# An RWKV-7 inversion on Trainium2: forward substitution in 8x8 blocks, joined to 16x16 by two products

## The chip, the cores and the metric

The kernel runs on one core of a Trainium2 chip. The metric is device time of one execution in microseconds (us), the median of several runs. The engines are TensorE (PE, its weight loads PEld), VectorE (DVE), ScalarE (ACT), GpSimd (POOL) and SyncE (SP, which issues the DMAs).

## The reference

Two layers of a hybrid decoder over 1024 tokens of width 1024. Each layer projects x, mixes tokens in three groups of heads (stick-breaking attention, latent attention, RWKV-7), projects back, and runs a gated FFN. What the change touches is the RWKV-7 mixer; its recurrence over time is

```python
def rwkv7_mixer(cols, mu, w0, w2, a0, a2, g2, k_k, k_a, r_k, gn_g, gn_b):
...
    def step(state, inp):
        r_t, w_t, k_t, v_t, kk_t, a_t = inp
        sa = jnp.einsum('bhvk,bhk->bhv', state, -kk_t)
        state = (state * w_t[:, :, None, :] + sa[..., None] * (kk_t * a_t)[:, :, None, :]
                 + v_t[..., None] * k_t[:, :, None, :])
        return state, jnp.einsum('bhvk,bhk->bhv', state, r_t)
...
    _, ys = lax.scan(step, init, (tm(rh), tm(wh), tm(kh), tm(vh), tm(kk), tm(ah)))
```

The kernel computes it in chunks of 64 tokens. Inside a chunk the dependence of each `sa` on earlier ones is a 64x64 triangular system, one for each chunk and head. The kernel inverts these unit triangular matrices.

## The kernel before

Matmuls with weights are three products in split precision (`mm3`, L205 to L207): `whi` and `wlo` are the high and low part of a weight tile, made by L200 (ScalarE) and L201 (VectorE).

`phase_a` holds the part around the change. For each of four feature tiles `ft` of 128 features (two heads) it projects k, then r, then v. Such a projection (`proj_rw`) has two halves of 512 tokens; each half is 24 matmuls into a PSUM tile `psmm`, of which there are three buffers, and is evacuated by L306 (ScalarE), then L310 or L308 and L311 (VectorE), which mixes each token with the one before it. L311 is the last large reader of the buffer. `rw_prep` and `rw_stage1` turn k, r, v into the operands of the chunks: L619 scales k, L643 and L644 make the masked operand that L668 transposes, L669 transposes v beside it, L649 and L653 make the operand that L676 transposes, and L689 and L690 mask the products of L684 into `Aa` and `RB`.

After two feature tiles `Aa` holds the A of 64 systems, and `rw_inv` inverts them; there are two such inversions in a layer, four in all. `rw_inv` is a generator. It copies the diagonal 32x32 blocks (L726, two pieces), transposes them so that each partition holds a whole block (L729), and inverts each 32x32 block on VectorE by rows. Before the change, forward substitution runs for t = 1 to 15 on the two 16x16 diagonal blocks at once: `mul` (L731) multiplies row t of A with the rows already known, `red` (L732) sums. Then the 16x16 block below the diagonal is joined by two products in four pieces each (first into `M`, then into `T`). `pd` holds the elementwise products. L752 transposes the result (`T11`), L761 on TensorE starts the join of 32x32 blocks to 64x64, with L780 and L792 after it, and L768 transposes once more.

What sets the order: a scheduler fixes each engine's order from the order of the program's text, with a few shifts of priority per helper. `step(n)` takes n pieces of `rw_inv`, up to its n-th next `yield`, into the text. The first inversion of a layer starts at ft = 2: six pieces after k's projection, six after r's, the rest after v's. The second runs beside `rw_chain(0, ...)`, the recurrence over chunks (L848 to L870), three pieces for each of its steps.

Of the kernel before, what the change touches and what calls it, by code (L numbers as in the profile page):

```python
# [69 lines left out]
class Body:  # L70
# [640 lines left out]
    def rw_inv(self, st, tp, Aa):  # L711
        nc = self.nc
        v32 = lambda t: t.rearrange("p (a b) -> p a b", b=32)
        LA = v32(self.t(tp, [P, S], "LA"))
        T = v32(self.t(tp, [P, S], "T"))
        pd = self.t(tp, [P, S], "pd")
        pd3 = v32(pd)
        M = self.t(tp, [P, 16, 16], "M")
# [11 lines left out]
        blk = lambda ap, off, dims: bass.AP(tensor=ap.tensor, offset=ap.offset + off, ap=[list(ap.ap[0])] + [list(d) for d in dims])  # L730
        mul = lambda o, x, y: nc.vector.tensor_tensor(o, x, y, op=ALU.mult)  # L731
        red = lambda o, x: nc.vector.tensor_reduce(o, x, axis=AX.X, op=ALU.add)  # L732
        for t in range(1, 16):
            pr = pd[:, : 2 * t * t].rearrange("p (b j i) -> p b j i", b=2, j=t)
            mul(pr, blk(LA, t * 32, [[528, 2], [0, t], [1, t]]), blk(T, 0, [[528, 2], [1, t], [32, t]]))
            red(blk(T, t * 32, [[528, 2], [1, t]]), pr)
            if t % 3 == 0:
                yield
        for j0 in range(0, 16, 4):
            ni = 16 - j0  # L740
            pr = pd[:, : 16 * 4 * ni].rearrange("p (t j i) -> p t j i", t=16, j=4)
            mul(pr, blk(LA, 512 + j0, [[32, 16], [0, 4], [1, ni]]), blk(T, j0 * 32 + j0, [[0, 16], [1, 4], [32, ni]]))
            red(M[:, :, j0 : j0 + 4], pr)
            yield
        for t0 in range(0, 16, 4):
            ni = t0 + 4
            pr = pd[:, : 4 * 16 * ni].rearrange("p (t j i) -> p t j i", t=4, j=16)
# [510 lines left out]
```

## Time and profile before

| | |
|---|---|
| median of 3 runs | 3023.79 us (3023.44 to 3026.31) |
| the profiled execution | 3025.69 us, its span 3024.0 us |
| TensorE busy | 2913.1 us (96%) |
| VectorE busy | 1727.8 us (57%) |
| ScalarE busy | 1074.8 us (36%) |
| GpSimd busy | 230.8 us (8%) |

The profile is of one execution. Its page gives busy times, the span in slices and the chain of work that ended last; behind the page stands the trace, in which each instruction has its start, its duration and the idle time before it. The span is 1.69 us shorter than the time of its execution. Busy time is not the time that an engine costs: only where the others wait for it does it lengthen the span. Granted clock is the share of TensorE's full clock.

### The profile page before, as it was taken

How to read it: one execution, taken by the hardware profiler on the slowest of the kernel's cores; microseconds unless marked ns; L12 is line 12 of the kernel's file. 1: busy time of each engine (PE TensorE's matmuls, PEld its weight loads, DVE VectorE, ACT ScalarE, POOL GpSimd, SP SyncE). 2: the span in 40 equal slices, each digit the busy share in tenths (PEclk: the TensorE clock that was granted, in tenths of full speed). 3: DMA queues.
4: the chain of work that ended last, by engine and by line, in shares of the span. 5: the costliest groups of instructions: out<-in, count | busy, mean ns of one | idle time of the engine just before them, and what ended most of it. 6: DMA issues, size and time to landing. Idle time of an engine off the chain costs nothing.

```text
span 3024.0 us, 41845 instructions
## 1 busy us (share of the span) xinstructions
PE 2913.1 (96%) x16572; PEld 2322.0 (77%) x16572; DVE 1727.8 (57%) x2857; ACT 1074.8 (36%) x1833; POOL 230.8 (8%) x308
## 2 busy tenths in 40 slices
PE   8999999889999999999999999999899999999998
PEld 6777777667888888888877777776678888888887
DVE  4568665886544444344645677568965443434437
ACT  5454454762211112121254644457612111212120
POOL 0001122030000000000000011210300000000000
PEclk9999999999999999999999999999999999999999
DMA  4353666324411111111124446562244111111111
GB/s 135 91 157 102 209 193 203 92 82 137 167 56 42 42 43 55 49 56 49 63 77 125 127 133 207 177 213 66 90 145 163 42 42 42 56 49 55 50 49 56
DMA packets 338260, 301.78 MB, mean 100 GB/s; under 512 B 24200, under 2 KB 302992, under 8 KB 338064
## 3 DMA queue, kind: packets, MB, share of 16 engines
q1 hardware_dynamic: 338064, 299.11, 32.6%
q8 instruction: 131, 2.15, 0.3%
q14 instruction: 65, 0.53, 0.1%
HBM read 208.87 MB, written 90.18 MB: 99 GB/s over the span
## 4 chain that ended last, share of the span: by engine, by line
PE 76%; DVE 10%; issue 8%; ACT 3%; DMA 3%; POOL 1%; SPq 0%; POOLq 0%; DVEq 0%; ACTq 0%
PE psmm L207 16%; PE psmm L206 16%; PE psmm L205 16%; PE psps L205 5%; PE psps L206 5%; PE psps L207 5%; PE pspa L848 2%; DVE pd L731 1%; PE pspi L792 1%; PE psmt L216 1%; DMA LA<-xxd 1%; DVE T L732 1%; PE pspa L684 1%; ACT pd L726 0%; DVE mexp L400 0%
## 5 line engine op out<-in xcount | busy, mean ns | idle before, releaser
L207 PE MATMUL psmm<-xTh,wlo 128*128 128x512 f32 x2144 | 849.1, 396 | 0.0
L205 PE MATMUL psmm<-xTh,whi 128*128 128x512 f32 x2144 | 847.0, 395 | 0.0
L206 PE MATMUL psmm<-xTl,whi 128*128 128x512 f32 x2144 | 846.8, 395 | 0.0
L200 ACT CAST whi<-raw 128x1024 fp32r<-128x1024 f32 x152 | 160.0, 1053 | 1062.1 <-PE psmm L206 1048.6
L205 PEld LDWEIGHTS psmm<-xTh,whi 128*128 128x128 f32 x2144 | 404.0, 189 | 88.6 <-issue 6.1
L206 PEld LDWEIGHTS psmm<-xTl,whi 128*128 128x128 f32 x2144 | 404.2, 189 | 87.9 <-issue 4.6
L207 PEld LDWEIGHTS psmm<-xTh,wlo 128*128 128x128 f32 x2144 | 404.2, 189 | 87.6 <-issue 4.2
L201 DVE TENSOR_TENSOR wlo<-raw,whi 128x1024 fp32r<-128x1024 f32 x152 | 185.6, 1221 | 456.7 <-ACT whi L200 440.4
L1060 DVE TENSOR_TENSOR y<-y,psps 128x512 f32<-128x512 f32 x288 | 196.5, 687 | 171.1 <-PE psps L207 171.0
L205 PE MATMUL psps<-wdh,hh 128*128 128x512 f32 x672 | 266.7, 397 | 0.0
L206 PE MATMUL psps<-wdl,hh 128*128 128x512 f32 x672 | 262.9, 391 | 0.0
L207 PE MATMUL psps<-wdh,hl 128*128 128x512 f32 x672 | 259.6, 391 | 0.0
L205 PEld LDWEIGHTS psps<-wdh,hh 128*128 128x128 f32 x672 | 126.1, 188 | 36.8 <-ACT hh L200 5.9
L923 POOL TENSOR_TENSOR lsm<-lsm,small 128x1 f32<-128x1 f32 x32 | 29.3, 915 | 1629.9 <-DVE lsm L922 1629.9
L207 PEld LDWEIGHTS psps<-wdh,hl 128*128 128x128 f32 x672 | 126.2, 188 | 26.9
L206 PEld LDWEIGHTS psps<-wdl,hh 128*128 128x128 f32 x672 | 126.2, 188 | 25.4
L1035 DVE TENSOR_TENSOR cv<-cv,psmm 128x1024 f32<-128x1024 f32 x44 | 53.8, 1222 | 136.6 <-PE psmm L207 131.7
L201 DVE TENSOR_TENSOR wdl<-raw,wdh 128x1024 fp32r<-128x1024 f32 x42 | 51.5, 1226 | 88.2 <-ACT wdh L200 88.2
L1030 ACT ACTIVATE cv<-cv 128x1024 f32<-128x1024 f32 x44 | 46.7, 1061 | 115.8 <-DVE cv L1029 115.8
L848 PE MATMUL pspa<-RBl,PSl 128*128 128x128 f32 x512 | 72.0, 286 | 11.1 <-ACT QC L851 5.3
L848 PEld LDWEIGHTS pspa<-RBl,PSl 128*128 128x128 f32 x512 | 64.6, 195 | 19.3 <-ACT QC L851 8.3
L206 PE MATMUL psmm<-wol,whi 128*128 128x512 f32 x192 | 76.6, 399 | 1.6 <-DVE wol L201 1.6
(444 smaller groups left out, 4504.7 us busy)
## 6 DMA issues: line engine op xcount, KB each, us to landing
raw<-in_ffn_w_up_dram SPq DMA_DIRECT2D x88, 512.0 KB
raw<-in_w_in_dram SPq DMA_DIRECT2D x44, 512.0 KB
raw<-in_ffn_w_down_dram SPq DMA_DIRECT2D x44, 512.0 KB
rbd<-RB SPq DMA_DIRECT2D x64, 256.0 KB
PSl<-psd SPq DMA_DIRECT2D x32, 512.0 KB
RBl<-rbd SPq DMA_DIRECT2D x32, 512.0 KB
psd<-Vz SPq DMA_DIRECT2D x64, 128.0 KB
xxd<-X SPq DMA_DIRECT2D x64, 128.0 KB
```

The lines of the kernel that those rows point to most:

```text
L200: self.nc.scalar.copy(hi, src)
L201: (eng or self.nc.vector).tensor_tensor(lo, src, hi.bitcast(F32), op=ALU.subtract)
L205: mm(out, lh, rh, start=start, stop=False)
L206: mm(out, lh, rl, start=False, stop=False)
L207: mm(out, ll, rh, start=False, stop=stop)
L216: nc.tensor.transpose(pt[:, k * P : k * P + P], xt[:, kk * P : kk * P + P], self.ident)
L684: ms.append(nc.tensor.matmul(pAs[h][:, cc * P : cc * P + P], flat(BK[hr, 2 * g + cc // 2, cc % 2]), AR[hr, :, 2 * g + cc // 2, cc % 2, :], ...
L731: mul = lambda o, x, y: nc.vector.tensor_tensor(o, x, y, op=ALU.mult)
L848: nc.tensor.matmul(pQ[:, f, e, :], PSh[:, f, h, e, :], RBh[:, f, h, e, :], start=True, stop=True)
L1030: nc.scalar.activation(cv, cv, AF.Gelu)
L1035: nc.vector.tensor_tensor(cv, cv, pg, op=ALU.mult)
L1060: nc.vector.tensor_tensor(y[:, i, hs], y[:, i, hs], ps, op=ALU.add)
```

## The change

Substitution runs for t = 1 to 7 on the four 8x8 diagonal blocks at once. Two products then make the 8x8 block below the diagonal in each of the two 16x16 blocks, each product in two halves b (one for each 16x16 block): A's lower left block times the upper inverse into `M`, then the lower inverse times `M` into `T`. The join from 16x16 to 32x32 and all that follows stay. An inversion has 38 instead of 46 multiplies and reductions on VectorE, and 21 instead of 22 pieces: substitution had yields behind t = 3, 6, 9, 12 and 15, and now behind t = 3 and 6 and behind each of the new products. Below the edit lines move down by nine (L752 becomes L761, L761 becomes L770).

```diff
--- before.py
+++ after.py
@@ -730,12 +730,21 @@
         blk = lambda ap, off, dims: bass.AP(tensor=ap.tensor, offset=ap.offset + off, ap=[list(ap.ap[0])] + [list(d) for d in dims])
         mul = lambda o, x, y: nc.vector.tensor_tensor(o, x, y, op=ALU.mult)
         red = lambda o, x: nc.vector.tensor_reduce(o, x, axis=AX.X, op=ALU.add)
-        for t in range(1, 16):
-            pr = pd[:, : 2 * t * t].rearrange("p (b j i) -> p b j i", b=2, j=t)
-            mul(pr, blk(LA, t * 32, [[528, 2], [0, t], [1, t]]), blk(T, 0, [[528, 2], [1, t], [32, t]]))
-            red(blk(T, t * 32, [[528, 2], [1, t]]), pr)
+        for t in range(1, 8):
+            pr = pd[:, : 4 * t * t].rearrange("p (b j i) -> p b j i", b=4, j=t)
+            mul(pr, blk(LA, t * 32, [[264, 4], [0, t], [1, t]]), blk(T, 0, [[264, 4], [1, t], [32, t]]))
+            red(blk(T, t * 32, [[264, 4], [1, t]]), pr)
             if t % 3 == 0:
                 yield
+        prs = [pd[:, 512 * b : 512 * b + 512].rearrange("p (t j i) -> p t j i", t=8, j=8) for b in range(2)]
+        for b in range(2):
+            mul(prs[b], blk(LA, 528 * b + 256, [[32, 8], [0, 8], [1, 8]]), blk(T, 528 * b, [[0, 8], [1, 8], [32, 8]]))
+            red(M[:, 8 * b : 8 * b + 8, 0:8], prs[b])
+        yield
+        for b in range(2):
+            mul(prs[b], blk(T, 528 * b + 264, [[32, 8], [0, 8], [1, 8]]), blk(M, 128 * b, [[0, 8], [1, 8], [16, 8]]))
+            red(blk(T, 528 * b + 256, [[32, 8], [1, 8]]), prs[b])
+        yield
         for j0 in range(0, 16, 4):
             ni = 16 - j0
             pr = pd[:, : 16 * 4 * ni].rearrange("p (t j i) -> p t j i", t=16, j=4)
```

The scheduler's order moves with it. The first place is VectorE in the first inversion of a layer, at ft = 2 of layer 1. `psmm_2031` (`psmm_2029` after) is the second half of r, `psmm_2082` (`psmm_2076`) the first of v, `q_388` the operand of L668, `T_1919`, `M_1921` and `pd_1920` are the inversion's. Before:

```order
L731 TENSOR_TENSOR pd_1920<-LA_1918,T_1919 128x162
L732 TENSOR_REDUCE T_1919<-pd_1920 128x2x9
L731 TENSOR_TENSOR pd_1920<-LA_1918,T_1919 128x200
L732 TENSOR_REDUCE T_1919<-pd_1920 128x2x10
L308 TENSOR_TENSOR pst_2002<-pst_2002,small_15_95 128x1
L311 SCALAR_TENSOR_TENSOR pst_2002<-psmm_2031,pv_67_288,pst_2002 128x511
L731 TENSOR_TENSOR pd_1920<-LA_1918,T_1919 128x242
L619 SCALAR_TENSOR_TENSOR kk_1955<-pst_1861,pv_67_288,kk_1955 128x1024
L732 TENSOR_REDUCE T_1919<-pd_1920 128x2x11
L643 SCALAR_TENSOR_TENSOR q_388_2364<-kk_1955,q_386_2357 128x4x63
L731 TENSOR_TENSOR pd_1920<-LA_1918,T_1919 128x288
L644 TENSOR_SCALAR q_388_2364<-kk_1955 128x4
```

After:

```order
L732 TENSOR_REDUCE T_1919<-pd_1920 128x4x7
L731 TENSOR_TENSOR pd_1920<-LA_1918,T_1919 128x512 x2
L732 TENSOR_REDUCE M_1921<-pd_1920 128x8x8 x2
L731 TENSOR_TENSOR pd_1920<-T_1919,M_1921 128x512 x2
L732 TENSOR_REDUCE T_1919<-pd_1920 128x8x8 x2
L619 SCALAR_TENSOR_TENSOR kk_1953<-pst_1861,pv_67_288,kk_1953 128x1024
L308 TENSOR_TENSOR pst_2000<-pst_2000,small_15_95 128x1
L311 SCALAR_TENSOR_TENSOR pst_2000<-psmm_2029,pv_67_288,pst_2000 128x511
L731 TENSOR_TENSOR pd_1920<-LA_1918,T_1919 128x1024
L310 TENSOR_SCALAR small_15_95<-psmm_2076,pv_67_288 128x1
L732 TENSOR_REDUCE M_1921<-pd_1920 128x16x4
L311 SCALAR_TENSOR_TENSOR pst_2075<-psmm_2076,pv_67_288,pst_2075 128x511
```

Before, t = 11 and later stand behind L311 of r's second half, and v's L311 follows a few rows behind the last one shown. Now both new products and L619 stand ahead of that L311, and a piece of the join to 32x32 stands between it and v's.

The second place is TensorE a little later, at the start of ft = 3. `psmm_2110` (`psmm_2104` after) is the second half of v, `psmm_2620` (`psmm_2612`) the first half of k of the next feature tile, `psmm_2640` the second half of it, `psmm_2718` the first half of r after that. Before:

```order
L207 MATMUL psmm_2110<-xTh_132,wlo_2077 128x512
L668 MATMUL pspa_2393<-ident_65,q_388_2364 128x128
L669 MATMUL pspa_2393<-cent_84,pst_2081 128x128
L668 MATMUL pspa_2393<-ident_65,q_388_2364 128x128
L669 MATMUL pspa_2393<-cent_84,pst_2081 128x128
L205 MATMUL psmm_2620<-xTh_132,whi_2614 128x512
L206 MATMUL psmm_2620<-xTl_133,whi_2614 128x512
L207 MATMUL psmm_2620<-xTh_132,wlo_2615 128x512
```

After:

```order
L207 MATMUL psmm_2104<-xTh_132,wlo_2071 128x512
L205 MATMUL psmm_2612<-xTh_132,whi_2606 128x512
L206 MATMUL psmm_2612<-xTl_133,whi_2606 128x512
L205 MATMUL psmm_2640<-xTh_132,whi_2606 128x512
L206 MATMUL psmm_2640<-xTl_133,whi_2606 128x512
L205 MATMUL psmm_2718<-xTh_132,whi_2712 128x512
L206 MATMUL psmm_2718<-xTl_133,whi_2712 128x512
L668 MATMUL pspa_2385<-ident_65,q_388_2356 128x128
L669 MATMUL pspa_2385<-cent_84,pst_2075 128x128
L668 MATMUL pspa_2385<-ident_65,q_388_2356 128x128
L669 MATMUL pspa_2385<-cent_84,pst_2075 128x128
L207 MATMUL psmm_2612<-xTh_132,wlo_2607 128x512
```

Before, the transposes of L668 and L669 come at once, and then the next k half whole. Now the first two matmuls of three projection halves stand ahead of these transposes, and the products with `wlo` behind them. Layer 2 has the same two pieces of order. Layer 1's attention is also issued in another order than before, layer 2's is not.

## Rows read from the trace of the kernel before

**Rows 1.** Page, chain that ended last: share of the span by engine.
```profile
PE 76%; DVE 10%; issue 8%; ACT 3%; DMA 3%; POOL 1%; SPq 0%; POOLq 0%; DVEq 0%; ACTq 0%
```

**Rows 2.** Windows: length, busy (x) of PE, PEld, DVE, ACT, POOL; PEclk, DMA, GB/s.
```profile
250.00:275.00 25.00, 19.92 (x131) 14.34 (x132) 24.00 (x34) 5.89 (x13) 2.53 (x3) 0.93 0.41 114
...
1750.00:1775.00 25.00, 20.39 (x124) 15.16 (x123) 23.97 (x32) 6.31 (x13) 2.50 (x3) 0.93 0.32 91
```

**Rows 3.** Window of t = 8 to 15, second inversion, tile pd alone.
```profile
359.24:371.10 11.86, 0.00 (x0) 0.00 (x0) 8.77 (x16) 0.00 (x0) 0.00 (x0) 0.99 0.77 269
```

**Rows 4.** VectorE's timeline, second inversion: start, duration, engine, line, operation, out<-in.
```profile
358.60 0.34 DVE L731 TENSOR_TENSOR pd<-LA,T 128x98 f32<-128x98 f32 x1
358.97 0.26 DVE L732 TENSOR_REDUCE T<-pd 128x14 f32<-128x98 f32 x1
...
360.86 0.53 DVE L731 TENSOR_TENSOR pd<-LA,T 128x200 f32<-128x200 f32 x1
361.42 0.36 DVE L732 TENSOR_REDUCE T<-pd 128x20 f32<-128x200 f32 x1
...
379.56 1.08 DVE L731 TENSOR_TENSOR pd<-LA,T 128x512 f32<-128x512 f32 x1
...
383.23 0.68 DVE L732 TENSOR_REDUCE M<-pd 128x64 f32<-128x512 f32 x1
```

**Rows 5.** VectorE's timeline, first inversion of layer 1.
```profile
233.44 0.40 DVE L731 TENSOR_TENSOR pd<-LA,T 128x128 f32<-128x128 f32 x1
...
235.95 0.74 DVE L311 SCALAR_TENSOR_TENSOR pst<-psmm,pv,pst 128x511 f32<-128x511 f32 x1
...
237.13 1.29 DVE L619 SCALAR_TENSOR_TENSOR kk<-pst,pv,kk 128x1024 f32<-128x1024 f32 x1
...
241.17 0.76 DVE L311 SCALAR_TENSOR_TENSOR pst<-psmm,pv,pst 128x511 f32<-128x511 f32 x1
...
242.31 1.23 DVE L201 TENSOR_TENSOR wlo<-raw,whi 128x1024 fp32r<-128x1024 f32 x1
...
247.48 0.75 DVE L311 SCALAR_TENSOR_TENSOR pst<-psmm,pv,pst 128x511 f32<-128x511 f32 x1
248.14 2.08 DVE L731 TENSOR_TENSOR pd<-LA,T 128x1024 f32<-128x1024 f32 x1
...
250.72 1.23 DVE L732 TENSOR_REDUCE M<-pd 128x64 f32<-128x1024 f32 x1
...
272.63 2.12 DVE L752 STREAM_TRANSPOSE LA<-T 128x1024 f32<-128x1024 f32 x1
```

**Rows 6.** TensorE's timeline beside it; brackets: idle time before, releaser.
```profile
243.01 0.40 PE L207 MATMUL psmm<-xTh,wlo 128*128 128x512 f32 x1
...
254.05 0.66 PE L676 MATMUL pspq<-ident,q 128*128 128x128 f32 x4 [3.61 <-DVE q L653]
...
255.75 0.63 PE L207 MATMUL psmm<-xTh,wlo 128*128 128x512 f32 x1
256.17 0.63 PE L205 MATMUL psmm<-xTh,whi 128*128 128x512 f32 x1
...
258.31 0.40 PE L206 MATMUL psmm<-xTl,whi 128*128 128x512 f32 x1
258.54 0.39 PE L207 MATMUL psmm<-xTh,wlo 128*128 128x512 f32 x1
```

**Rows 7.** TensorE's waits, 243 to 288 us: total, times, longest.
```profile
PE pspq L698 <- DVE Aa L689: 0.7, 1, 0.7
PE pspi L761 <- DVE LA L752: 0.5, 1, 0.5
```

**Rows 8.** TensorE's waits, 284 to 352 us.
```profile
PE pspi L792 <- DMA LA<-xxd: 0.9, 1, 0.9
PE pspi L792 <- ACT T L793: 0.7, 1, 0.7
```

**Rows 9.** TensorE's waits, 352 to 440 us (chain 0, second inversion).
```profile
PE pspa L848 <- ACT QC L851: 2.2, 1, 2.2
```

## The prediction

> **What bounds the kernel now.** I read the chain of waits first: TensorE holds 76% of it, VectorE 10% [rows 1]. So the time is TensorE's work plus the places where it stands still, and an edit on VectorE counts only where TensorE waits for VectorE. The table of 25 us windows finds such a place: between 250 and 275 us VectorE is busy for 24.00 of 25 us, TensorE for 19.92 at a granted clock of 0.93, and in layer 2 the same picture stands at 1750 to 1775 [rows 2]. This is where the first inversion of a layer runs beside the projections of feature tile 2 (below: ft 2). TensorE's timeline shows the size: before L676 at 254.05 it idles 3.61 us for VectorE's q (L653), and then its matmuls start 0.42 apart (255.75, 256.17); from 258.31 they start 0.23 apart again (258.31, 258.54) [rows 6]. Of the two clock levels, 1.2 and 2.4 GHz, the first pace is that of the lower one. So some 4.2 us, 254.05 to 258.31, run at about half pace: 2.1 us are lost. Smaller waits follow: 0.7 for Aa (L689), 0.5 for the transposed T11 (L752) [rows 7], 0.9 and 0.7 at L792 [rows 8]. A layer's first inversion thus costs TensorE 3.6 + 2.1 + 0.5 + 0.7 + 1.6 = **8.5 us** now. There are four inversions: two such (one a layer), and two beside the recurrence of chain 0, where the longest wait, 2.2, is for ScalarE's QC [rows 9].
>
> **VectorE's work.** Removed are steps t = 8 to 15: eight multiplies and eight reductions, together 8.77 us [rows 3]. Steps 1 to 7 stay, each over twice the elements. The seventh goes from 98 to 196 elements; at 98 the pair costs 0.34 + 0.26, at 200 it costs 0.53 + 0.36 [rows 4], so this step grows by 0.29. The smaller ones grow by their elements at the same rate (98 elements more for 0.29; the other six add 182 between them, at 0.003 each): 0.55. Growth 0.85, between 0.3 (the last step alone) and 2.0 (seven times the last). Added are four multiplies of 512 elements and four reductions of 512 to 64: 4 x (1.08 + 0.68) = 7.04 [rows 4]. Net per inversion: -8.77 + 0.85 + 7.04 = -0.9, with the gaps of eight instructions fewer about -1.2. Four inversions take about 4.4 us off VectorE, 0.15% of the span. That alone is below 6 us (0.2%), about what a measurement of this kernel can tell from no change.
>
> **What the order moves.** The larger effect is where the new products stand. The first six pieces of the inversion run in step(6), ahead of the evacuations of r and v. Before, they end with t = 12, and the scheduler mixes t = 11 to 15 with the evacuations. Now they are the loading of A, t = 1 to 7 and both new products, and VectorE's order has all 7.04 us ahead of L311 of r's second half, and L619 too. Behind the waiting L311 stand two more evacuations, v's halves, each now behind a large product of the next join (1024 and 768 elements). TensorE needs all three: its new order puts two matmuls of each of the next three projection halves ahead of L668, and each half needs a PSUM buffer that one of the three L311 sets free (there are three). I walk VectorE through this, since it does not pause there. Neighbours overlap by 0.09 (L311 at 247.48 lasts 0.75, its successor starts at 248.14 [rows 5]); small steps between (L310, L643, L644), 0.1 to 0.5 a group, are estimates.
> - r, second half: t = 8 started at 233.44 [rows 5]. From there 0.85 + 7.04 + L619's 1.29 less nine overlaps: L311 at 241.8 instead of 235.95, its end 242.5.
> - v, first half: behind 2.08 + 1.23 (the 1024 pair): L311 at 245.6 instead of 241.17, end 246.4.
> - v, second half: behind the 768 pair, 2.5 by interpolation between the pairs of 512 and 1024, and a small step: 248.9 instead of 247.48, end 249.6.
> - q for L668: behind a 512 pair and three small steps: 251.7; it was ready ahead of wlo's start at 242.31. wlo takes 1.23 and ends at 252.9 instead of 243.5.
>
> TensorE comes free of v's last half at 243.24 (the matmul at 243.01 plus a step). Two matmuls to 243.7, then it waits for 246.4: 2.7. Two to 246.85, waits for 249.6: 2.75. Two to 250.05, waits for 251.7: 1.65. L668 and L669 to 252.15, waits for wlo at 252.9: 0.7. Sum 7.8, in place of 3.6. L653, second half, for which TensorE waited until 254.05, moves to about 259, but now TensorE has 25 matmuls (5.7 us, more at the low clock) ahead of L676, so that wait goes to nothing. What is late next is T11: its transpose ended at 274.75 [rows 5] and will end about 5 us earlier (in the new order the evacuations, the Aa masks of L689 and L690 and one wlo stand behind it), but TensorE's order now has L761 earlier too; I put the wait at 1.1 (as before, 0.5, up to 2), the wait for Aa behind the second transpose at 0.9 (0 to 1.5), those at L792 at 0.8 (0 to 1.6). The low clock I take once, 2.1, since the last idle time is followed by a long row of matmuls as at 254.05. After: 7.8 + 2.1 + 1.1 + 0.9 + 0.8 = 12.7. Less 8.5 gives **+4.2 a layer**, with ends at 2.6 (the later waits gone) and 5.6 (their upper ends, or half of the low clock again).
>
> **The second inversion of a layer** has no projections beside it. Its pieces come three at a time between chunks of chain 0, one piece fewer in all. VectorE's chain is 1.2 shorter; of that TensorE gets what is not covered by the 2.2 for QC, which no edit touches. I take -0.7, between -1.2 (all of it) and +1 (a chunk's evacuation behind a large product, half of a wait like that in rows 9).
>
> Layer 1's attention is also issued in another order by the scheduler; its work is the same. No row prices it: 0, with ends -2 and +2, about the longest single wait seen [rows 9].
>
> **Sum.** 2 x (4.2 - 0.7) = +7.0 us. The profiled execution took 3025.69 (span 3024.0 and 1.69 around it), 1.9 above the median of the runs, so it would become 3032.7, and the median 3023.79 becomes 3030.8. Range of this case: 2 x (2.6 - 1.2) - 2 = +0.8 to 2 x 5.6 + 2 = +13, 3024.6 to 3037.
>
> **Clock.** In the rows one idle time of 3.61 is followed by about 4.2 us at the lower level, and the granted clock of the whole window is 0.93 [rows 2, 6]; no row shows several short idle times in a row. The Trainium skill, page "TensorE: Matmul & The Clock Gate", section "A second HAM failure mode: psum-queue depth-cycling", tells of a kernel that paused briefly each time it cycled through PSUM buffers, so that the clock went up and down and throughput was lost in between. By that section the new waits for three buffers would be paid again in pace, and the sum would be that of rival B; by the row it is the 2.1 that I took.
>
> **Rivals.**
> - **B, the clock stays low.** If TensorE runs from 252.9 to L761 at the lower level, the some 44 large matmuls there lose 0.2 each [rows 6], 8.8 instead of 2.1, while the waits for T11 and Aa (2.0) are covered: +4.7 a layer more, 3030.8 + 9.4 = 3040. For it: three idle times within 10 us. Against: after 3.61 us of idling the pace came back within 4.2.
> - **C, the order moves nothing that counts (faster).** If VectorE gets the evacuations done in time, as it would if the new products overlapped other work, the change does only what its words say: VectorE reaches L653 1.2 earlier, the wait of 3.6 becomes 2.4, T11's 0.5 goes, and about 1 of the 2.1 at the low clock; with the second inversion's 0.7: 2 x 3.4 = 6.8 less, 3017. It decides if L311 of v's first half ends before TensorE needs it, 243.7. Against: VectorE is busy for 24 of 25 us there, and the order is fixed.
> - **D, given back.** The inversion ends about 5 us earlier. If this clears all later waits (T11, Aa, L792), the sum after is 9.9, +1.4 a layer, and the second inversion at its better end gives -1.2: 3024, no change.
>
> **Chances.** Forecast case 0.66 (0.38 of it above 6 us, 0.28 within), B 0.10, C 0.13, D 0.11. Slower by over 0.2%: 0.38 + 0.10 = 0.48; within: 0.28 + 0.11 = 0.39; faster: 0.13. The range 3021 to 3037 leaves out B and most of C, about 2 in 10; the forecast case's own range is 3024.6 to 3037.
>
> **What would show it.** In the profile after: VectorE's busy time some 4 us less; L311 of r's second half near 242 and three waits of TensorE for L311, L311 and L644 of about 2.7, 2.7 and 1.6 between 243 and 252, none for L653; the lower clock only once, around 253 to 257; T11's transpose ending near 270. Wrong would be: waits for L311 under 1 us (then C), matmuls at the 0.42 pace beyond 260 (then B), no waits at L761 and L792 (then D), or a difference that lies in attention, where I put nothing.

## The result and the profile after

The changed kernel takes 3047.01 us in the median (3039.79 to 3050.09), the kernel before 3024.61 beside it (3023.44 to 3026.31). The ratio is 1.0070, interval 1.0051 to 1.0090: slower, and by about three times what was forecast (3030.8, range 3021 to 3037). The profiled execution took 3045.18, its span 3043.4; before it was 3025.69 and 3024.0, so the two traces differ by 19.4 us. The page after, its span, its busy times and its chain of waits by engine:

```profile
span 3043.4 us, 41847 instructions
...
PE 2926.6 (96%) x16572; PEld 2330.4 (77%) x16572; DVE 1723.8 (57%) x2825; ACT 1074.6 (35%) x1833; POOL 233.1 (8%) x308
...
PE 75%; DVE 9%; issue 8%; DMA 3%; ACT 3%; POOL 1%; SPq 0%; POOLq 0%; DVEq 0%; ACTq 0%
```

VectorE is busy 4.0 us less than before (1727.8), as the change meant. TensorE is busy 13.5 us *more* (2913.1 before), with the same 16572 matmuls. That is the line to start from: two thirds of the loss are not waiting but work that takes longer. In the chain, the shares hardly differ from [rows 1].

Was the first inversion as forecast? VectorE's timeline after, the three L311 of [rows 5] (r's second half, v's two halves), q's last piece L644 and the transpose of T11:

```profile
239.65 0.80 DVE L311 SCALAR_TENSOR_TENSOR pst<-psmm,pv,pst 128x511 f32<-128x511 f32 x1
...
243.56 0.74 DVE L311 SCALAR_TENSOR_TENSOR pst<-psmm,pv,pst 128x511 f32<-128x511 f32 x1
...
246.90 0.75 DVE L311 SCALAR_TENSOR_TENSOR pst<-psmm,pv,pst 128x511 f32<-128x511 f32 x1
...
249.52 0.17 DVE L644 TENSOR_SCALAR q<-kk 128x4 f32<-128x4 f32 x1
...
264.77 2.16 DVE L761 STREAM_TRANSPOSE LA<-T 128x1024 f32<-128x1024 f32 x1
```

TensorE's timeline beside it, for comparison with [rows 6]:

```profile
244.45 0.47 PE L205 MATMUL psmm<-xTh,whi 128*128 128x512 f32 x1 [2.81 <-DVE pst L311]
...
247.79 0.77 PE L205 MATMUL psmm<-xTh,whi 128*128 128x512 f32 x1 [2.63 <-DVE pst L311]
...
249.74 0.47 PE L668 MATMUL pspa<-ident,q 128*128 128x128 f32 x1 [0.75 <-DVE q L644]
...
251.50 0.63 PE L205 MATMUL psmm<-xTh,whi 128*128 128x512 f32 x1
251.93 0.63 PE L206 MATMUL psmm<-xTl,whi 128*128 128x512 f32 x1
...
253.05 0.40 PE L206 MATMUL psmm<-xTl,whi 128*128 128x512 f32 x1
253.28 0.40 PE L207 MATMUL psmm<-xTh,wlo 128*128 128x512 f32 x1
...
257.17 0.60 PE L676 MATMUL pspq<-ident,q 128*128 128x128 f32 x4
...
266.99 1.20 PE L770 MATMUL pspi<-LA,Aa 32*32 32x32 f32 x64 [1.12 <-DVE LA L761]
```

The end of v's projection stands 2.2 us earlier here than before (0.3 earlier in `after_again`, a second run of the same program), so 2.2 is to be added: L311 at 241.8, 245.7 and 249.1, L644's last at 251.7. TensorE waits 2.81 and 2.63 for L311 and 0.75 for L644; none is left for L653 (L676 at 257.17 has no bracket). Matmuls start 0.43 apart at 251.50 and 0.23 apart from 253.05: the low clock once. The granted clock is at its lower level from 246.0 to 252.9, and TensorE works for 4.3 us of that (before: from 254.9 to 258.3, 3.4 us, all of it work). T11 makes TensorE wait 1.12.

Then where do 19 us come from? To see it I count the matmuls of projections (psmm from x) in TensorE's timelines, since both kernels have the same ones, and compare the times at which the same number is done. 624 stands at the end of v of ft 2, 850 just ahead of chain 0, 1104 at the last projection matmul of chain 1, 1120 at the start of the FFN, behind attention and the output projection. Differences of after and before over each stretch, in us:

| stretch (projection matmuls) | layer 1 | layer 2 |
|---|---|---|
| 624 to 850, first inversion | +1.2 | +0.4 |
| 850 to 1104, both chains and the second inversion | +10.1 | +7.7 |
| 1104 to 1120, rest of chain 1, attention, output projection | +1.8 | +0.2 |

The rest is the start of layer 1 (2.2 earlier) and of layer 2 (0.2 later). So the loss lies in the second stretch, where I had put -0.7; before, it is 144.4 and 144.5 us long. In layer 2 the work of TensorE in it is the same, in layer 1 it holds 16 more Y products (some 0.9). Of +10.1 in layer 1, waits are 3.0; S and Y products (L867, L875) cost 4.8 more, those 16 among them, projection matmuls 2.4 more, T11 products 0.6 more.

Layer 2 is another mixture. Its stretch, length, busy (x) of PE, PEclk, DMA, GB/s, before and after, and a piece of it after:

```profile
1857.71:2002.17 144.46, 139.21 (x1284) 0.99 0.66 208
```

```profile
1869.25:2021.45 152.20, 144.56 (x1284) 0.97 0.61 192
...
1928.77:1932.18 3.41, 3.41 (x26) 0.50 0.15 55
```

The granted clock is at its lower level for 10.2 us here, in three pieces like the last one, against 3.4 before; at half pace that is 3.4 of the +7.7. Waits are 2.4, and some 2 are left for slower work at the full clock. In layer 1 the clock goes the other way: none at the lower level after, 3.4 us before. Over the whole span the clock is no rival: it is 0.989 in the mean before and 0.986 after, but 0.985 in `x_first` below, which takes no longer than the kernel before.

Back in layer 1, this is TensorE at the same place towards the end of chain 1 in both kernels, after first:

```profile
496.30 0.33 PE L876 MATMUL pspq<-S,QC 128*64 128x64 f32 x2
496.56 0.50 PE L207 MATMUL psmm<-xTh,wlo 128*128 128x512 f32 x1
496.99 0.33 PE L876 MATMUL pspq<-S,QC 128*64 128x64 f32 x2
497.25 0.51 PE L205 MATMUL psmm<-xTh,whi 128*128 128x512 f32 x1
497.68 0.33 PE L876 MATMUL pspq<-S,QC 128*64 128x64 f32 x2
```

```profile
497.75 0.50 PE L207 MATMUL psmm<-xTh,wlo 128*128 128x512 f32 x1
498.09 0.39 PE L205 MATMUL psmm<-xTh,whi 128*128 128x512 f32 x1
498.32 0.40 PE L206 MATMUL psmm<-xTl,whi 128*128 128x512 f32 x1
498.56 0.39 PE L207 MATMUL psmm<-xTh,wlo 128*128 128x512 f32 x1
498.88 0.45 PE L867 MATMUL pspq<-S,QC 128*64 128x64 f32 x8
499.26 0.50 PE L205 MATMUL psmm<-xTh,whi 128*128 128x512 f32 x1
```

After, two S products and one projection matmul take turns: a pair and a matmul take 0.69 (496.30 to 496.99). Before, four projection matmuls in a row take 1.13 (497.75 to 498.88) and eight S products 0.38: by these, a pair and a matmul would be 0.10 + 0.28 = 0.38. Each turn costs 0.3. T11's products do the same to the chain in layer 2, after and then before:

```profile
1923.87 0.33 PE L884 MATMUL pspq<-S,QC 128*64 128x64 f32 x2
1924.13 0.24 PE L770 MATMUL pspi<-LA,Aa 32*32 32x32 f32 x2
1924.30 0.33 PE L884 MATMUL pspq<-S,QC 128*64 128x64 f32 x2
1924.56 0.24 PE L770 MATMUL pspi<-LA,Aa 32*32 32x32 f32 x2
```

```profile
1914.02 0.63 PE L761 MATMUL pspi<-LA,Aa 32*32 32x32 f32 x28
...
1915.48 0.97 PE L875 MATMUL pspq<-S,QC 128*64 128x64 f32 x16
```

Two Y products and two T11 products take 0.43; in long runs the pair and the pair are 0.11 (0.90 for 16 at 1915.48) and 0.04 (0.56 for 28): 0.28 lost. What is lost shows on the weight loads (PEld), after first:

```profile
496.30 0.19 PEld L876 LDWEIGHTS pspq<-S,QC 128*64 128x64 f32 x2 [0.37 <-ACT ys L893]
496.56 0.19 PEld L207 LDWEIGHTS psmm<-xTh,wlo 128*128 128x128 f32 x1
496.99 0.19 PEld L876 LDWEIGHTS pspq<-S,QC 128*64 128x64 f32 x2 [0.24 <-issue]
497.25 0.19 PEld L205 LDWEIGHTS psmm<-xTh,whi 128*128 128x128 f32 x1
```

```profile
497.75 0.19 PEld L207 LDWEIGHTS psmm<-xTh,wlo 128*128 128x128 f32 x1
497.86 0.19 PEld L205 LDWEIGHTS psmm<-xTh,whi 128*128 128x128 f32 x1
498.09 0.19 PEld L206 LDWEIGHTS psmm<-xTl,whi 128*128 128x128 f32 x1
```

Within a run of one kind the next load starts 0.11 after its predecessor's matmul and runs beside it (497.86 beside the matmul of 497.75). In the turns each load starts only with its own matmul, and PEld's idle time before it is put down to issue. The Trainium skill, page "TensorE: Matmul & The Clock Gate", section "The mechanism", says that a weight load is pulled ahead of matmuls in flight when it targets row groups that do not conflict, or the background weight buffer. Here the loads of projection matmuls, all over the same 128 rows, do run beside them, so of the two only the second can apply. That the overlap goes where the size of the tile changes (128x128, 128x64, 32x32) is what these rows show. A change of kind that keeps the size costs nothing, as L597 between projection matmuls after:

```profile
260.27 0.39 PE L207 MATMUL psmm<-xTh,wlo 128*128 128x512 f32 x1
260.50 0.39 PE L597 MATMUL pspy<-q,bonesr 128*128 128x512 f32 x1
260.73 0.39 PE L205 MATMUL psmm<-xTh,whi 128*128 128x512 f32 x1
```

The steps are 0.23 and 0.23, as in a row of projections.

The order of the kernels shows the same without a run. In each layer, between projection matmul 850 and 1104, I count how often TensorE's order changes the kind of work (projection, S and Y, RBl, T11, Z, the transposes and so on): 146 and 143 times before, **185 and 155** after. Changes of the tile size alone are 100 and 96 before, 142 and 112 after. The scheduler made that of the new VectorE chain.

### The profile page after: what moved, and what is told of

It reads as the page before. It is cut to its first block, busy times and chain, and to the rows that moved or that the text cites. A ratio compares the mean times of both kernels' runs of the same rounds, so it can differ in the third digit from the quotient of the medians.

```text
span 3043.4 us, 41847 instructions
## 1 busy us (share of the span) xinstructions
PE 2926.6 (96%) x16572; PEld 2330.4 (77%) x16572; DVE 1723.8 (57%) x2825; ACT 1074.6 (35%) x1833; POOL 233.1 (8%) x308
## 4 chain that ended last, share of the span: by engine, by line
PE 75%; DVE 9%; issue 8%; DMA 3%; ACT 3%; POOL 1%; SPq 0%; POOLq 0%; DVEq 0%; ACTq 0%
PE psmm L205 16%; PE psmm L206 16%; PE psmm L207 16%; PE psps L205 5%; PE psps L206 5%; PE psps L207 5%; PE pspa L857 2%; DVE pd L731 1%; PE pspi L801 1%; PE psmt L216 1%; PE pspa L684 1%; DMA PSl<-psd 1%; PE pspq L884 0%; DVE T L732 0%; DMA xt<-in_x_dram 0%
## 5 line engine op out<-in xcount | busy, mean ns | idle before, releaser
L205 PEld LDWEIGHTS psmm<-xTh,whi 128*128 128x128 f32 x2144 | 403.9, 188 | 101.0 <-issue 17.8
```

The source lines that it names most:

```text
L205: mm(out, lh, rh, start=start, stop=False)
```

## The experiments

Theory A: the loss is TensorE's order in the stretch of the chains. Rival B: it is the late evacuations of the first inversion, and their echo. Rival C: the new products make the second inversion itself longer. All ratios are against runs of the kernel before that were taken beside them.

**The change in one inversion of each layer.** `x_first` has it in the first alone, `x_second` in the second alone:

```diff
+        if not st:        # x_second: if st
             for t in range(1, 8):
...
+        else:
+            for t in range(1, 16):
```

> The new substitution only in the first inversion of each layer (the one beside the projections); the second keeps the 16x16 substitution of before. Equal-work stretches of the two traces give the first inversion +3.2 - 2.0 = about +1 us a layer, and +8 a layer for the second inversion and chain 1. In this kernel's TensorE order no T11 product alternates with the chain's S products. Theory A (the loss is made in the second inversion and in the recurrence, by TensorE's order there): 3024.6 + 2 to 6 = 3027 to 3031. Rival B (it is made by the late evacuations of the first inversion, and all that follows is their echo): close to the changed kernel, 3040 to 3047.

3023.25, ratio 0.9995 (0.9986 to 1.0003): no slower than the kernel before, below what either theory had.

> The new substitution only in the second inversion of each layer; the first is that of before, so r's and v's evacuations stand where they stood. In TensorE's order T11 products and S products of the chain alternate, 22 changes between the two kinds. Theory A: most of the loss is here, 3036 to 3042. Rival B: at or below the kernel before, 3020 to 3025.

3034.30, ratio 1.0026 (1.0017 to 1.0036). Rival B falls: with the late evacuations of the changed kernel and the second inversion of before (`x_first`) there is no loss. But theory A's sum falls too, as the parts give -2 and +9, not +22. What the two do not have is the order of both together: 143 and 138 changes of kind, and 156 and 151, against 185 and 155. The 22 alternations that I expected of `x_second` are not those of T11: in its trace T11 products change places with the chain's 4 times, the products at the end of the inversion (L792 before) 20 times.

**Mending the order of the changed kernel.** `a_kept` holds the T11 products together; `a_evac` raises the evacuations; `a_evac_kept` does both:

```diff
+                    with self.tc.high_priority(offset=300):
                         nc.tensor.matmul(psM[r2, f, :], ...
...
         ps = self.proj_h(hi, lo, h)
+            with self.tc.high_priority(offset=100):
                 nc.scalar.activation(d[:, o : o + 512], ps, ...
```

> The changed kernel with the 32 small products of T11 (psM) at a higher priority, so that each group of them stays together in TensorE's order: changes between T11 products and S products fall from 32 to 4. In the trace of the changed kernel eight such alternations of two and two in layer 2 took 0.43 us each instead of about 0.15. Theory A, in its form that changing between small products costs time: 2 to 3 us a layer less, 3040 to 3043. Rival: alternation costs nothing, 3047 within 2.

3037.28, ratio 1.0038 (1.0026 to 1.0051): 10 us less than the changed kernel, more than expected; 14 changes of kind fewer in each layer do not give so much at the price below.

> The changed kernel with the evacuations of the RWKV projections (L306, L308, L310, L311) at a higher priority, so that L311 of r and v stands ahead of or among the new products. TensorE's order then has as many projection matmuls ahead of chain 1 as before (1061 instead of 1036 at its first product), 15 instead of 40 left for its end. Rival B (evacuations and their echo): the waits of 2.8 + 2.6 a layer are gone and nearly the whole loss with them, 3024 to 3028. Theory A (second inversion, alternations, which stay at 38): some 8 us come back, 3036 to 3041.

3034.18, ratio 1.0024 (1.0015 to 1.0033). Each mending alone takes away about half of the loss of 22 us or a little more. The priority of `a_evac` holds for all four feature tiles, though: of the 10.6 us that its trace is shorter than that of the changed kernel, 5.3 lie ahead of the first inversions' stretches, and `b_evac` below shows what it is worth without the change.

> The changed kernel with both orders mended: evacuations of the RWKV projections at a higher priority, and the T11 products kept together. In TensorE's order changes between T11 and S products fall from 32 to 6, changes between S products and projection matmuls from 129 to 92 (before 91), and 1064 instead of 1036 projection matmuls stand ahead of chain 1 (before 1061). VectorE's work is the new one everywhere. Theory A (the loss is TensorE's order, not the arithmetic): at or a little below the kernel before, 3018 to 3026. Rival C (the new products themselves lengthen the second inversion's path): not below 3032, since the two single mendings gave 3037 and 3034.

3028.04, ratio 1.0007 (0.9998 to 1.0016): with the new arithmetic in all four inversions, some nine tenths of the loss are gone, though 2 us short of theory A's range. Rival C falls: the stretch of the chains is 142.5 and 142.4 long, less than before. Part of what was won is no mending, as the next runs show.

**Evacuations alone.** `b_evac` and `b_evaclow` are the kernel before with offset 100 and -100 on the same lines; `x_first_evac` is `x_first` with 100.

> The kernel before with the evacuations at a higher priority: the priority alone, without the new substitution, as a base for the mended kernels. TensorE waits 3.6 us a layer for L653 before; the priority moves L653 little. Theory A: 3019 to 3026 (total of changes between kinds on TensorE 2108 instead of 2164). Rival B: below 3019, as the evacuations are what counts.

3017.15, ratio 0.9973 (0.9964 to 0.9982): faster than before, lower than theory A's range, as rival B said. Its waits for L653 and L644 in the first inversion are

```profile
PE pspa L669 <- DVE q L645: 1.1, 1, 1.1
PE pspq L677 <- DVE q L654: 0.9, 1, 0.9
```

(lines are one further down), 0.9 instead of 3.6 for the operand of L676. The gain stands elsewhere, however: the stretch of the first inversion is +0.2 and -2.2, that ahead of it 3.7 and 1.8 shorter, the chains 4.0 and 4.1 shorter, the third stretch 3.0 and 4.0 longer. So the priority is worth 8 us to a kernel that lacks the change, and against `b_evac` the mended `a_evac_kept` is 10.9 us slower. Of that, its trace has 3.8 and 7.0 in the first inversions. The loss is not undone there; with the evacuations ahead of the new products, part of it has moved to the first inversion.

> The kernel before, its arithmetic untouched, with the evacuations at a lower priority, so that L311 of r and v stands behind the substitution. TensorE's order then has the same count of projection matmuls at each step of the chain as the kernel with the new substitution in the first inversion alone (855 ahead of chain 0), 0 changes between T11 and S products and 93 between S products and projections. Theory A: late evacuations alone cost little by the end of the layer, 3024 to 3030. Rival B: they cost what the prediction said, 4 us a layer, 3032 to 3036.

3033.19, ratio 1.0027 (1.0016 to 1.0037), as rival B said. In its trace the first stretch is 6.8 and 5.0 us longer, the chains 1.9 and 4.7 shorter. Late evacuations do have the price that I put on them where the inversion does not end earlier for it.

> New substitution in the first inversion alone, with the evacuations at a higher priority. TensorE's order has the fewest changes between S products and projection matmuls of all (85), none between T11 and S products, and no projection matmul left for the end of chain 1. Theory A: below both kernels, 3016 to 3021. Rival B (late evacuations cost some 3 us a layer): also a gain on the 3023 of the same kernel without the priority, of 4 to 6 us. Rival D (priority moves nothing that counts): 3023.

3028.82, ratio 1.0015 (1.0006 to 1.0024): theory A's miss. The stretch of the chains is indeed 8.3 and 4.2 us shorter than before, but two things stand against it. The first stretch is 6.8 and 4.9 longer, since with the evacuations ahead q comes late; the same in `a_evac`, TensorE's waits there:

```profile
PE pspa L669 <- DVE q L645: 3.7, 1, 3.7
PE pspy L685 <- DVE q L659: 1.5, 1, 1.5
```

And projections that are done sooner are missing at the end of chain 1: the third stretch is 10.9 and 2.9 longer. The number of changes counts only as long as the chain has projections beside it.

**One number.** `a_s0` and `b_s80` change only the priority of the chain's S and Y products:

```diff
-    "rw_chain_s": 40,
+    "rw_chain_s": 0,     # after: a_s0;   before: 80, b_s80
```

> The changed kernel once more, beside the others of this call on the same chip, as their base: 3040 to 3050 (3047 before).

3047.48, ratio 1.0074 (1.0060 to 1.0087).

> The changed kernel with one number changed: the priority of the chain's S and Y products (rw_chain_s) 0 instead of 40. Arithmetic, first inversion and evacuations are as in the changed kernel. Counted in its order, TensorE changes the kind of its work (projection, S, RBl, T11 and so on) 139 and 138 times between projection matmul 850 and 1104 of the two layers, instead of 185 and 155 (before 146 and 143). Over the ten traces so far this stretch grows by 0.2 to 0.3 us for each change. Theory A (the loss is these changes of kind): 63 changes fewer, 13 to 19 us less, 3026 to 3034. Rival C (the new products and the late evacuations are the loss): 3040 to 3050.

3030.76, ratio 1.0024 (1.0014 to 1.0034): 17 us come back with the arithmetic, the first inversion and the evacuations of the changed kernel, and the stretch of the chains is 145.0 and 146.2 long, about as before. What this number is worth to the kernel before was not measured.

> The kernel before, arithmetic untouched, with one number changed: priority of rw_chain_s 80 instead of 40. Its first inversion is ordered as before; in the stretch of the chains TensorE changes kind 187 and 184 times instead of 146 and 143. Theory A: 82 changes more at 0.2 to 0.3 us, 16 to 25 us more, 3041 to 3050, with none of the new arithmetic. Rival C: 3020 to 3030, since nothing of the inversion is changed.

3038.45, ratio 1.0048 (1.0036 to 1.0061): 13 us are lost without the change, 3 us less than the least expected. Its TensorE takes turns between RBl and Y products:

```profile
483.44 1.16 PE L848 MATMUL pspa<-RBl,PSl 128*128 128x128 f32 x8
484.53 0.45 PE L867 MATMUL pspy<-S,QC 128*64 128x64 f32 x8
...
491.63 0.33 PE L875 MATMUL pspq<-S,QC 128*64 128x64 f32 x2
491.89 0.49 PE L848 MATMUL pspa<-RBl,PSl 128*128 128x128 f32 x2
492.31 0.33 PE L875 MATMUL pspq<-S,QC 128*64 128x64 f32 x2
```

Two and two take 0.68 (491.63 to 492.31). Eight RBl products in a row take 1.09 (483.44 to 484.53), so a pair 0.27, and a pair of Y products 0.11: 0.30 a turn are lost here too. In the stretch of the chains it loses 3.1 and 3.5 us for 41 changes each, its waits being 1.4 and 1.8 shorter, and then 4.6 and 1.8 in the third stretch, for which the count has no reason; TensorE's waits there are 2.7 and 2.8 longer.

**A version that beats both.** `b_evac_q120` is `b_evac` with `"rw_chain_q": 120` instead of 80.

> A version meant to beat both kernels: arithmetic of before, evacuations at a higher priority (3017 alone), and the priority of rw_chain_q 120 instead of 80. Changes of kind fall from 138 and 137 to 119 and 122. Theory A: 34 changes fewer, 7 to 10 us less than 3017, 3007 to 3012, if the one step more of chain 1 that has no projection beside it costs nothing; with that step's waits (2 to 4 us a layer) 3012 to 3017. Rival: order counts no more than this, 3017.

3012.45, ratio 0.9959 (0.9947 to 0.9972). Its page:

```profile
span 3004.8 us, 41871 instructions
...
PE 2904.5 (97%) x16572; PEld 2319.1 (77%) x16572; DVE 1728.3 (58%) x2857; ACT 1073.2 (36%) x1833; POOL 236.5 (8%) x308
```

TensorE is busy 8.6 us less than before with the same matmuls. Its stretch of the chains is 11.3 and 10.2 shorter, and 7.5 and 3.1 of it are given back behind it, where chain 1 has one step more without a projection beside it.

The stretch of the chains in all profiled executions, with the changes of kind counted in the order (one layer each, us):

| kernel | changes | length |
|---|---|---|
| b_evac_q120 | 119, 123 | 133.1, 134.2 |
| a_evac_kept | 136, 135 | 142.5, 142.4 |
| b_evac | 138, 137 | 140.5, 140.4 |
| a_s0 | 139, 138 | 145.0, 146.2 |
| x_first | 143, 138 | 143.1, 141.9 |
| b_evaclow | 143, 138 | 142.6, 139.8 |
| before | 146, 143 | 144.4, 144.5 |
| x_second | 156, 151 | 148.2, 146.7 |
| a_evac | 161, 158 | 147.5, 148.1 |
| a_kept | 171, 141 | 151.0, 145.3 |
| after | 185, 155 | 154.6, 152.2 |
| after_again | 185, 155 | 158.2, 147.7 |
| b_s80 | 187, 184 | 147.6, 147.9 |

Without `b_evac_q120` and `x_first_evac`, whose projections run out early, a line through these 24 points rises by 0.21 us a change (correlation 0.81). The single turns above give 0.28 to 0.3 for a turn there and back, 0.15 a change. Much of the scatter is the clock and waits: layer 2 of `after` and `after_again`, the same program, are 4.5 apart, and of that 3.4 are the clock (10.2 us at the lower level against 3.4), 1.5 waits. Less TensorE's waits and half of the time at the lower level, the line rises by 0.18 (correlation 0.94); with changes of the tile size counted in place of the kind, by 0.17 (0.96). So of the +17.8 that the changed kernel has in this stretch, 58 changes of the tile size more make some 10, by that price; waits are 5.4, the clock 1.7, and 0.9 is work that stood behind it before. The profiled executions of `a_s0`, `x_first_evac`, `b_evaclow` and `b_evac_q120` lie 5 to 7 us off their medians: their stretches tell where the time goes, not how much the median moves.

## Why the prediction was wrong

**VectorE's work** was right: -4.4 forecast, -4.0 measured.

**The moved evacuations** were right in place: 241.8, 245.6, 248.9 and 251.7 forecast, 241.8, 245.7, 249.1 and 251.7 measured. The waits were 2.81 + 2.63 + 0.75 and none for wlo, 6.2 instead of 7.8: TensorE was at the low clock from the second wait on, as its pace of 0.43 at 251.50 shows, came to L668 later and so waited less. The low clock came once, as forecast, and the 4.3 us of work in it cost 2.2 (2.1 forecast); but the 2.1 that I had read for the kernel before are 1.7, since its granted clock is low for 3.4 us and not 4.2. Rival B of the prediction, by which it would stay, did not occur. The Trainium skill, page "TensorE: Matmul & The Clock Gate", section "A second HAM failure mode: psum-queue depth-cycling", which I had weighed, tells of a clock that goes up and down with such pauses; here it fell once beside three waits.

**What is late next** in the first inversion was half right. T11's wait is 1.12 (1.1 forecast). But in layer 1 the waits for Aa fell to 0.2 (0.9 forecast) and those of [rows 8] at L792 are gone (0.8 forecast), with two new ones of 0.4 and 0.5 in their place. TensorE's waits in this stretch went from 6.5 to 8.7 and, in layer 2, from 7.0 to 8.1; the stretch grew by 1.2 and 0.4, and not by 4.2. That the inversion ends earlier and gives back later waits was rival D's mechanism, and it acts in this place alone. Why the stretch grows by less than its waits stays open.

**The range** was added up wrongly at its ends: without the waits for Aa and at L792 the first inversion is +2.5 and not +2.6, with the upper ends of those two and of T11's it is +6.5 and not +5.6, and the +1 of the second inversion is missing from the upper end. Put right, the upper end is 3041; 3047 lies beyond that too.

**The second inversion** is the step that failed: -0.7 a layer, with ends at -1.2 and +1, against +10.1 and +7.7 for its stretch. I took VectorE's chain as the thing that moves and TensorE's order as given, and asked only which waits get shorter. But the scheduler puts TensorE's order anew over the whole phase. 26 fewer projection matmuls stand ahead of chain 0, and 40 instead of 15 are left for the end of chain 1. In layer 1 they take turns with S products there one by one: changes between projections and the chain's S and Y products are 74 instead of 43, in layer 2 only 45 instead of 40. In both layers T11 takes turns with Y products. That costs TensorE busy time, which a search for waits does not find. The counts of projections are not the cause by themselves, as `x_first` has the same 26 fewer ahead of chain 0 and `a_s0` the same 40 left; the turns are (50 and 48 in `a_s0`). `a_s0`, which undoes most of it with one number, and `b_s80`, which does it to the kernel before, show that it is the order. In layer 2 the clock and waits weigh more than the turns. The new waits in the stretch, 3.0 and 2.4 us, are for S (L879) and for the first PSl of chain 1, which the second inversion writes:

```profile
PE pspa L857 <- DMA PSl<-psd: 1.2, 1, 1.2
```

Before, no wait of TensorE is listed between 425 and 503 us.

**Layer 1's attention**, 0 with ends at 2, took +1.8 with the rest of chain 1, within the ends.

So the direction was right for a reason that carried a tenth of it. What stays open is why the scheduler alternates more when both inversions are changed than the sum of either, why layer 2's clock fell three times in the changed kernel, and why `b_s80` waits longer behind the chains.

## What to carry to other kernels

Where a scheduler sets the order, a change on one engine is a change of every other engine's order, so compare the orders over the whole phase, on the bound engine first, and count how often it changes the kind of its work. Most of such a loss stands in busy time, where a list of waits does not show it. And compare a mended kernel with the old one that has the same mending: a gain that the mending gives to any kernel is not a loss undone. A priority can be worth more than the arithmetic: one number gave back 17 us, and two priorities on the old arithmetic beat the kernel before by 12.7.

## What the runs showed of the hardware

A change between matmuls of different tile size on TensorE costs about 0.15 us: 0.69 for a pair of 128x64 products and a projection matmul that are 0.38 in long runs, 0.43 for two and two that are 0.15, 0.68 for two 128x128 and two 128x64 that are 0.38. The loads of weights no longer run beside the matmuls ahead of them there. A change of kind that keeps the tile size costs nothing (0.23 to L597 and 0.23 from it).

In the first inversion of layer 1 the granted clock fell to its lower level once. In the kernel before it did so 0.8 us behind an idle time of 3.61, for 3.4 us; in the changed kernel 1.6 us behind one of 2.81, within that of 2.63, for 6.8 us (10.2 in `after_again`). In the changed kernel's second layer it fell three times in the stretch of the chains, for 3.4 us each: twice right behind idle times of 2.02 and 2.23, and once (at 1928.8) with no idle time above 0.3 in the 18 us ahead of it.
